# A chunked delta-rule recurrence: the pair's inverse multiplied into B and into the readout's scores once, two product bursts per step

## The chip, the cores and the metric

The kernel runs on one core of one Trainium2 chip. TensorE (PE) multiplies, VectorE (DVE), ScalarE (ACT) and GpSimd (POOL) do the rest, SyncE (SP) issues most transfers. The metric is device time in microseconds (us) of one execution; what counts is the median of several runs.

## The reference

One layer of a hybrid backbone over 256 latent and 256 context tokens, model width 2048, float32. A modulated RMSNorm is followed by one input projection (2048 to 16512 columns); its parts feed a neighbourhood attention, a multi-scale pooling and a bidirectional RWKV-7 mixer, each times a SiLU gate, then through a branch projection, a sigmoid merge gate, one output projection, a gated residual and a last RMSNorm. The change is in the third mixer:

```python
def step(S, inp):                       # 16 heads of 64 x 64, two directions
    rt, vt, wt, kt, at, bt = inp
    sa = jnp.einsum('bhij,bhj->bhi', S, at)
    S = S * wt[:, :, None, :] + sa[..., None] * bt[:, :, None, :] + vt[..., None] * kt[:, :, None, :]
    return S, jnp.einsum('bhij,bhj->bhi', S, rt)
...
y_c, s_ctx_end = wkv_scan(r_c, v_c, *dirs_c[d], s0, reverse=(d == 1))
y_l, _ = wkv_scan(r_l, v_l, *dirs_l[d], s_ctx_end, reverse=(d == 1))
```

The state runs over the 256 context tokens and then over the 256 latent ones; only the latent outputs are used.

## The kernel before, in words

**The dense work.** Weights come as tiles of 512 KB (`raw`, three buffers). ACT rounds half a tile to `whi` (line 576), DVE takes the rest `wlo` (line 577; five buffers of each), and PE multiplies three times for float32 accuracy: columns of the input projection into `d` (line 871; 256 columns wide for latent tokens alone, 512 for both), merge gates and branch projections into `dg` (lines 582 to 584), the output projection into `o`.

**The recurrence** takes two heads at a time, a *pair*, eight pairs in all. Tokens go in chunks of 64: four of the context (q = 0) and four of the latents (q = 1), both directions `d` at once, the two heads as `par`. For each pair `features` makes decays, keys and rates; its scan writes the tile `up` (lines 140, 142), ACT makes exponentials `E` (lines 151 to 154) and `G` (lines 158, 159) of it. `scores` makes the products of the chunks, `inverse` inverts the diagonal blocks of 32 on DVE through a DRAM round trip, and `merge` joins two blocks of 32 to the inverse of 64, `AT` (products `mp`, lines 339 and 347). `chain` then makes eight steps of three bursts of products: `px` (line 374), copied to `xs`; `pu` = inverse times `xs` (line 388), copied to `SV`; and `pS`, the next state (line 398), which DVE multiplies by the decay `G`, with the old state times the decay (`sg`, on POOL). In the four latent steps `py` sums the output from `SV` and state (lines 382, 411). `readout` normalises.

**The order of the work.** PE's order is written out. `Order` runs generators ("streams": one pair's recurrence, attention, pooling, gates); each yields the PE time of what it has just issued and how long its results take, in us, or the name of an event to wait for. Between the bursts of the streams that are ready, `Order.run` puts dense products, at least 0.6 us of them at a time. The next pair's stream is added when this pair's merge has been issued; its second half of features waits for this pair's chain. The other engines' orders follow from the scheduler's priorities. The gate for the residual (`mg`, `pg`, line 1115) is loaded and multiplied near the end; the third branch's projection needs the last pair's output, which goes through DRAM (`bs`, read back as `bh` and `bl`).

**Memory.** PSUM has tags `f` (features, scores; two banks), `m` (merge, `py`, readout; one bank), `c` (chain; one bank), `d` (dense; two) and `s`, `o` (attention). In SBUF the tags `up` and `E` have one buffer each, shared by features, inverse and merge.

Of the kernel before, what the change touches and what calls it, by code (L numbers as in the profile page):

```python
# [9 lines left out]
F32 = mybir.dt.float32  # L10
F32R = mybir.dt.float32r
AF = mybir.ActivationFunctionType
ALU = mybir.AluOpType
# [6 lines left out]
class Rwkv:  # L20
# [90 lines left out]
    def features(s, p, q, zk, zv, T, psp, ptag, gates):  # L111


        nc, fp = s.nc, s.fp
# [11 lines left out]
        k = s.mix(zk, 0, p, "k" + nm)  # L126
# [7 lines left out]
        for d in range(2):  # L134
            nc.scalar.activation(ta[:, d], psa[:, d], AF.Tanh, bias=s.dcol(64 + 8 * d, p), scale=0.5)
        yield 1.0, 2.2

        up = fp.tile([128, 8, 65], F32, tag="up", name=f"up{nm}")
# [9 lines left out]
        h = 0.5 * C  # L148
# [175 lines left out]

    def merge(s, p, psp, ptag):

        nc = s.nc
        at = [s.AT[p, q][:, 0:4].rearrange("p c d t -> p (c d) t") for q in range(2)]
        DN = s.fp.tile([128, 16, 32], F32, tag="up", name=f"DN{p}")
        P = s.fp.tile([128, 16, 32], F32, tag="E", name=f"mP{p}")  # L330
        ps1 = psp.tile([128, 16, 32], F32, tag=ptag, name=f"mp1{p}")
        rr = [(slice(64 * h, 64 * h + 32), slice(64 * h + 32, 64 * h + 64)) for h in range(2)]
        for q in range(2):
            for r1, r2 in rr:
                nc.vector.transpose(DN[r1, 8 * q:8 * q + 8], at[q][r1, :, 0:32])
        yield 0.0, 4.4
        for i in range(16):
            for h, (r1, r2) in enumerate(rr):
                nc.tensor.matmul(ps1[r2, i], at[i // 8][r1, i % 8, 32:64], DN[r1, i], start=True, stop=True,
                                 tile_position=(64 * h, 64 * h + 32))  # L340
        for h, (r1, r2) in enumerate(rr):
            (nc.scalar.copy if h else nc.vector.tensor_copy)(P[r2], ps1[r2])
        yield 0.9, 2.4
        ps2 = psp.tile([128, 16, 32], F32, tag=ptag, name=f"mp2{p}")
        for i in range(16):
            for h, (r1, r2) in enumerate(rr):
                nc.tensor.matmul(ps2[r1, i], P[r2, i], at[i // 8][r2, i % 8, 32:64], start=True, stop=True,
                                 tile_position=(64 * h + 32, 64 * h))
        for q in range(2):
            for h, (r1, r2) in enumerate(rr):  # L350
                (nc.scalar.copy if h else nc.vector.tensor_copy)(at[q][r1, :, 32:64], ps2[r1, 8 * q:8 * q + 8])
        yield 0.9, 2.2

    def chain(s, p, psp, ptag, psy, ytag, y, mark):
        nc = s.nc
        G = s.G[p]
# [4 lines left out]
        for i in range(8):  # L361
            q, w = i // 4, i % 4
            EO, AT, BKT, SV = s.EO[p, q], s.AT[p, q], s.BKT[p, q], s.SV[p, q]
            cs = (w, 3 - w)
            gs = ((i, 0), (i + 1, 1))
            if 0 < i < 7:
                sg = s.fp.tile([128, 2, 64], F32, tag="sg", bufs=2, name=f"sg{p}_{i}")
                for par in range(2):
                    for d in range(2):
                        nc.gpsimd.tensor_scalar(sg[hv[par], d], SV[hv[par], par, w, d], G[hv[par], gs[d][0], d:d + 1], None, ALU.mult)  # L370
            px = psp.tile([128, 2, 64], F32, tag=ptag, name=f"px{p}_{i}")
            for d in range(2):
                for par in range(2):
                    nc.tensor.matmul(px[hv[par], d], EO[:, par, d, cs[d], :], SV[:, par, w, d], start=True, stop=True,  # L374
                                     tile_position=(0, 64 * par))
            xs = s.fp.tile([128, 2, 64], F32, tag="xs", bufs=2, name=f"xs{p}_{i}")
            nc.vector.tensor_copy(xs, px)
            if q:
                py = psy.tile([128, 2, 64], F32, tag=ytag, name=f"py{p}_{i}")
                for d in range(2):  # L380
                    for par in range(2):
                        nc.tensor.matmul(py[hv[par], d], SV[:, par, w, d], EO[:, par, d, 4 + cs[d], :], start=(d == 0), stop=False,
                                         tile_position=(0, 64 * par), skip_group_check=True)
            yield (0.9 if q else 0.45), (1.0 if q else 1.6)
            pu = psp.tile([128, 2, 64], F32, tag=ptag, name=f"pu{p}_{i}")
            for d in range(2):
                for par in range(2):
                    nc.tensor.matmul(pu[hv[par], d], AT[hv[par], cs[d], d, :], xs[hv[par], d], start=True, stop=True)  # L388
            for par in range(2):
                (nc.scalar.copy if par else nc.vector.tensor_copy)(SV[hv[par], par, w], pu[hv[par]])  # L390
            yield 0.4, 2.0
            if i < 7:
# [7 lines left out]
                for par in range(2):  # L400
                    for d in range(2):
                        g = G[hv[par], gs[d][0], d:d + 1]
                        o = SV2[hv[par], par, j % 4, d]
                        if i:
                            nc.vector.scalar_tensor_tensor(o, pS[hv[par], d], g, sg[hv[par], d], ALU.mult, ALU.add)
                        else:
                            nc.vector.tensor_scalar(o, pS[hv[par], d], g, None, ALU.mult)  # L407
# [122 lines left out]
def hybrid_block(ctx, tc, x, cx, w_ms, w_st, w_in, w_mg, w_br, w_out, pool_w, icnt, wa, bias, rows, params, out, dbg=None):  # L530
    nc = tc.nc
# [349 lines left out]
    with ExitStack() as mx:  # L881
# [120 lines left out]
        def rwkv(p):  # L1002
# [20 lines left out]
            yield from R.inverse(p)  # L1023
            yield from R.merge(p, psm, "m")
            if p < 7:
                O.add(rwkv(p + 1), 2 + p + 1)
            if p:
                yield f"rw{p - 1}"
# [83 lines left out]
        def gate_out(cc, gs):  # L1112
            yield 0.0, 4.0
            pg = psn.tile([P, 512], F32, tag="o", name=f"pg{cc}")
# [239 lines left out]
```

## Time and profile before

| | |
|---|---|
| median of 3 runs | 1567.87 us (1566.26 to 1570.13) |
| profiled execution | 1565.28 us, its span 1563.6 us |
| PE busy | 1510.7 us, 97% of the span |
| DVE, ACT, POOL busy | 72%, 51%, 16% |
| granted PE clock | 0.991 of full speed on average |
| HBM traffic | 183 GB/s over the span |

How to read it: a group of instructions stands with its line, its engine, its output and inputs, their shapes, the count, then busy time, mean ns of one, and the idle time before it with what ended it. A float32 product stands as two records in the trace, so four products of a burst read x8. The timeline gives start and duration in us. PE's products are pipelined, so what a product costs is read from one start to the next, not from its duration.

### The profile page before, as it was taken

The numbers are of one execution on the slowest core, as the hardware profiler recorded it, in microseconds if no ns is written. First come the engines' busy times: TensorE is split into PE (matmuls) and PEld (weight loads), VectorE is DVE, ScalarE is ACT, GpSimd is POOL, SyncE is SP. The second block draws the span as 40 slices with busy tenths as digits, with TensorE's granted clock in tenths as the row PEclk, the third lists the DMA queues.
The fourth block names the chain that finished last, engine by engine and source line by source line (L and its number), as shares of the span: only waits on it lengthen the run. The fifth ranks groups of instructions, "written<-read, shape, count | busy, mean of one in ns | idle before, by whom it ended". The sixth has DMA issues, their size and how long they took to land.

```text
span 1563.6 us, 32275 instructions
## 1 busy us (share of the span) xinstructions
PE 1510.7 (97%) x12256; PEld 1199.3 (77%) x12256; DVE 1133.1 (72%) x2602; ACT 798.5 (51%) x1599; POOL 248.5 (16%) x438
## 2 busy tenths in 40 slices
PE   7999999999999999999999999999999999998998
PEld 5667878798877897788789877877896665667787
DVE  5345788788887877886887768778777775566664
ACT  4224663575465546544664556356646633334453
POOL 2332010150022022201230230023023200210000
PEclk9999999999999999999999999999999999999999
DMA  9996445545532464243355524523566698878863
GB/s 391 348 330 223 144 143 169 163 152 179 173 126 91 137 180 147 95 132 122 100 175 159 179 77 132 175 104 118 167 198 211 202 299 274 268 242 262 267 207 111
DMA packets 217811, 288.21 MB, mean 184 GB/s; under 512 B 62516, under 2 KB 176308, under 8 KB 213048
## 3 DMA queue, kind: packets, MB, share of 16 engines
q1 hardware_dynamic: 210160, 275.66, 54.3%
q10 hardware_dynamic: 7496, 10.50, 1.9%
q8 instruction: 96, 1.57, 0.4%
q14 instruction: 59, 0.48, 0.1%
HBM read 264.34 MB, written 21.50 MB: 183 GB/s over the span
## 4 chain that ended last, share of the span: by engine, by line
PE 86%; DVE 5%; DMA 4%; ACT 2%; issue 2%; SPq 0%; ACTq 0%; POOL 0%; DVEq 0%; POOLq 0%
PE d L871 36%; PE dg L582 9%; PE dg L583 7%; PE dg L584 7%; PE acc L793 2%; PE o L582 2%; DMA raw<-in_w_br 2%; PE o L584 2%; PE o L583 2%; PE px L374 2%; PE acc L799 1%; PE acc L796 1%; PE pu L388 1%; PE pS L398 1%; PE psm L693 1%
## 5 line engine op out<-in xcount | busy, mean ns | idle before, releaser
L576 ACT CAST whi<-raw 128x512 fp32r<-128x512 f32 x584 | 354.0, 619 | 388.7 <-PE d L871 169.5
L577 DVE TENSOR_TENSOR wlo<-raw,whi 128x512 fp32r<-128x512 f32 x584 | 400.4, 698 | 131.3 <-ACT whi L576 100.0
L871 PE MATMUL d<-hh,whi 128*128 128x256 f32 (+1 forms) x1184 | 367.5, 330 | 1.1 <-ACT mth L967 1.1
L871 PE MATMUL d<-hl,whi 128*128 128x256 f32 (+1 forms) x1184 | 359.3, 323 | 0.0
L871 PEld LDWEIGHTS d<-hh,whi 128*128 128x128 f32 x1184 | 225.4, 190 | 24.3 <-issue 2.9
L871 PE MATMUL d<-hh,wlo 128*128 128x256 f32 (+1 forms) x1184 | 241.4, 323 | 0.0
L871 PEld LDWEIGHTS d<-hl,whi 128*128 128x128 f32 x1184 | 225.9, 191 | 16.2 <-issue 0.2
L871 PEld LDWEIGHTS d<-hh,wlo 128*128 128x128 f32 x1184 | 183.0, 191 | 16.9 <-issue 0.7
L370 POOL TENSOR_SCALAR sg<-SV,G 64x64 f32<-64x64 f32 x192 | 111.4, 586 | 355.7 <-DVE SV L407 194.1
L582 PE MATMUL dg<-whi,hh 128*128 128x512 f32 x384 | 164.0, 427 | 0.4 <-DVE gnag L911 0.3
L584 PE MATMUL dg<-wlo,hh 128*128 128x512 f32 x384 | 150.7, 392 | 0.8 <-DVE wlo L577 0.6
L583 PE MATMUL dg<-whi,hl 128*128 128x512 f32 x384 | 150.6, 392 | 0.0
L582 PE MATMUL dg<-whi,bh 128*128 128x512 f32 x192 | 83.3, 434 | 10.4 <-ACT whi L576 3.0
L582 PEld LDWEIGHTS dg<-whi,hh 128*128 128x128 f32 x384 | 72.0, 187 | 23.6 <-issue 5.9
L584 PEld LDWEIGHTS dg<-wlo,hh 128*128 128x128 f32 x384 | 72.1, 188 | 17.9 <-DVE wlo L577 1.6
L583 PEld LDWEIGHTS dg<-whi,hl 128*128 128x128 f32 x384 | 72.4, 188 | 10.0 <-issue 0.2
L584 PE MATMUL dg<-wlo,bh 128*128 128x512 f32 x192 | 77.5, 404 | 0.5 <-DVE wlo L577 0.5
L583 PE MATMUL dg<-whi,bl 128*128 128x512 f32 x192 | 77.3, 403 | 0.5 <-DMA bl<-bs 0.5
L309 DVE TENSOR_TENSOR iM<-iA,iT 128x126 f32<-128x126 f32 (+22 forms) x248 | 63.6, 257 | 17.3 <-DMA iA<-dA 10.7
L311 DVE TENSOR_TENSOR iT<-iT,iM 128x126 f32<-128x126 f32 (+22 forms) x248 | 62.8, 253 | 6.6
L806 ACT ACTIVATE hh<-xT,md 128x256 fp32r<-128x256 f32 x32 | 17.5, 593 | 90.5 <-DVE md L717 90.5
L1283 DVE TENSOR_TENSOR wl<-raw,wh 128x512 fp32r<-128x512 f32 x64 | 41.3, 686 | 25.2 <-ACT wh L1282 25.0
(329 smaller groups left out, 2488.6 us busy)
## 6 DMA issues: line engine op xcount, KB each, us to landing
raw<-in_w_in SPq DMA_DIRECT2D x244, 512.0 KB, 3.6
wm<-in_w_ms SPq DMA_DIRECT2D x32, 1024.0 KB, 7.0
raw<-in_w_br SPq DMA_DIRECT2D x48, 512.0 KB, 5.5
wg<-in_w_mg SPq DMA_DIRECT2D x64, 256.0 KB, 4.2
raw<-in_w_out SPq DMA_DIRECT2D x32, 512.0 KB, 4.5
wst<-in_w_st SPq DMA_DIRECT2D x16, 448.0 KB, 7.9
sl<-in_bias SPq DMA_DIRECT2D x32, 128.0 KB, 3.0
iA<-dA SPq DMA_DIRECT2D x16, 256.0 KB, 5.4
```

Source lines behind the costliest of these rows:

```text
L309: nc.vector.tensor_tensor(m, A[:, st:st + 1, st + 1:32].to_broadcast([128, ni, nt]), T[:, 0:ni, st:st + 1].to_broadcast([128, ni, nt]), AL ...
L311: nc.vector.tensor_tensor(T[:, 0:ni, st + 1:32], T[:, 0:ni, st + 1:32], m, ALU.add)
L370: nc.gpsimd.tensor_scalar(sg[hv[par], d], SV[hv[par], par, w, d], G[hv[par], gs[d][0], d:d + 1], None, ALU.mult)
L374: nc.tensor.matmul(px[hv[par], d], EO[:, par, d, cs[d], :], SV[:, par, w, d], start=True, stop=True, tile_position=(0, 64 * par))
L576: nc.scalar.copy(hi, src)
L577: nc.vector.tensor_tensor(lo, src, hi.bitcast(F32), ALU.subtract)
L582: nc.tensor.matmul(acc, a[0], b[0], start=start, stop=False)
L583: nc.tensor.matmul(acc, a[1], b[0], start=False, stop=False)
L584: nc.tensor.matmul(acc, a[0], b[1], start=False, stop=stop)
L793: mm = nc.tensor.matmul(acc[i], shi[:, c], hh[j], start=(j == 0), stop=False)
L871: nc.tensor.matmul(box[0], w[m >= 8][:, 128 * i:128 * i + 128], x, start=(v == 0 and m == 0), stop=(v == 3 and m == 11))
L1283: nc.vector.tensor_tensor(l, r, h.bitcast(F32), ALU.subtract)
```

## The change

`merge` now makes, beside the inverse, the same inverse transposed, as full tiles of 64 x 64 (`An`, 16 a pair): two transposes of 128 partitions on DVE in place of four of 32, two memsets on POOL, and added products (`d2`, `P`) beside the old ones, which one DVE and one ACT copy of 32 x 512 bring to `An`. Then 32 products `pw` a pair multiply `An` into `BKT`, through PSUM tags `m` and `c`, and four copies write `BKT` back. In `chain` the burst `pu` and the copy `xs` are gone: `px` is copied to `SV` directly, and the next state uses the multiplied `BKT`. In the first step 16 products `pz` multiply `An` into the readout's scores `AT[:, 4:8]`, which ACT copies back. `sg` is one product for both directions. The next pair's stream is added before the merge; its features stop after their first part until the merge is issued (`merge{p}`). `gate_out` yields 6.5 us for 4.0. What the yields declare of PE time changes with it.

```diff
+        if q == 0 and p:
+            yield f"merge{p - 1}"
...
-    def merge(s, p, psp, ptag):
+    def merge(s, p, psp, ptag, psc, ctag):
...
-        DN = s.fp.tile([128, 16, 32], F32, tag="up", name=f"DN{p}")
-        P = s.fp.tile([128, 16, 32], F32, tag="E", name=f"mP{p}")
+        An = s.fp.tile([128, 16, 64], F32, tag="E", name=f"An{p}")
+        P = s.fp.tile([128, 16, 32], F32, tag="up", name=f"mP{p}")
...
-                nc.tensor.matmul(ps2[r1, i], P[r2, i], at[i // 8][r2, i % 8, 32:64], start=True, stop=True,
-                                 tile_position=(64 * h + 32, 64 * h))
+                d2 = at[i // 8][r2, i % 8, 32:64]
+                nc.tensor.matmul(ps2[r2, i], d2, P[r2, i], start=True, stop=True, tile_position=(64 * h + 32, 64 * h + 32))
+                nc.tensor.matmul(ps2[r1, i], P[r2, i], d2, start=True, stop=True, tile_position=(64 * h + 32, 64 * h))
+        for h, (r1, r2) in enumerate(rr):
+            (nc.scalar.copy if h else nc.vector.tensor_copy)(An[r2, :, 0:32], ps2[r2])
...
-        yield 0.9, 2.2
+        yield 1.4, 2.4
+        for q in range(2):
+            pw = (psp, psc)[q].tile([128, 2, 4, 64], F32, tag=(ptag, ctag)[q], name=f"pw{p}_{q}")
+            for d in range(2):
+                for c in range(4):
+                    for par in range(2):
+                        nc.tensor.matmul(pw[hv[par], d, c], An[hv[par], 8 * q + 2 * c + d], s.BKT[p, q][hv[par], par, d, c],
+                                         start=True, stop=True)
+            for par in range(2):
+                (nc.scalar.copy if par else nc.vector.tensor_copy)(s.BKT[p, q][hv[par], par], pw[hv[par]])
+        s.An = An
+        yield 1.8, 2.4
...
                 sg = s.fp.tile([128, 2, 64], F32, tag="sg", bufs=2, name=f"sg{p}_{i}")
+                g2 = G.rearrange("p a b -> p (a b)")[:, 2 * i:2 * i + 4:3]
                 for par in range(2):
-                    for d in range(2):
-                        nc.gpsimd.tensor_scalar(sg[hv[par], d], SV[hv[par], par, w, d], G[hv[par], gs[d][0], d:d + 1], None, ALU.mult)
+                    nc.gpsimd.tensor_tensor(sg[hv[par]], SV[hv[par], par, w], g2[hv[par]].unsqueeze(2).to_broadcast([64, 2, 64]), ALU.mult)
...
-            xs = s.fp.tile([128, 2, 64], F32, tag="xs", bufs=2, name=f"xs{p}_{i}")
-            nc.vector.tensor_copy(xs, px)
...
-            yield (0.9 if q else 0.45), (1.0 if q else 1.6)
-            pu = psp.tile([128, 2, 64], F32, tag=ptag, name=f"pu{p}_{i}")
-            for d in range(2):
-                for par in range(2):
-                    nc.tensor.matmul(pu[hv[par], d], AT[hv[par], cs[d], d, :], xs[hv[par], d], start=True, stop=True)
             for par in range(2):
-                (nc.scalar.copy if par else nc.vector.tensor_copy)(SV[hv[par], par, w], pu[hv[par]])
-            yield 0.4, 2.0
+                (nc.scalar.copy if par else nc.vector.tensor_copy)(SV[hv[par], par, w], px[hv[par]])
+            if i == 0:
+                pz = psy.tile([128, 8, 64], F32, tag=ytag, name=f"pz{p}")
+                at = s.AT[p, 1][:, 4:8].rearrange("p c d t -> p (c d) t")
+                for k in range(8):
+                    for par in range(2):
+                        nc.tensor.matmul(pz[hv[par], k], s.An[hv[par], 8 + k], at[hv[par], k], start=True, stop=True)
+                nc.scalar.copy(at, pz)
+            yield (0.9 if q or i == 0 else 0.45), (2.0 if q or i == 0 else 2.3)
...
-            yield from R.merge(p, psm, "m")
             if p < 7:
                 O.add(rwkv(p + 1), 2 + p + 1)
+            yield from R.merge(p, psm, "m", psc, "c")
+            O.mark(f"merge{p}")
...
         def gate_out(cc, gs):
-            yield 0.0, 4.0
+            yield 0.0, 6.5
```

PE's queue from the end of pair 5's merge into its first step, before (left out between the bursts are the dense products `d15` of 128 x 512: twelve, nine and six, the last six around eight of the next pair's features):

```order
L347 MATMUL mp25_12728<-AT5_1_11861,mP5_12612 32x32 x16
...
L374 MATMUL px5_0_12784<-SV5_0_11325,EO5_0_11322 64x64 x4
...
L388 MATMUL pu5_0_12816<-xs5_0_12789,AT5_0_11323 64x64 x4
...
L398 MATMUL pS5_0_12857<-SV5_0_11325,BKT5_0_11324 64x64 x4
```

The same place in the changed kernel; the first and the last of the twelve dense products between the merge and `pw` are shown, and lines count 19 or so higher:

```order
L353 MATMUL mp25_12671<-mP5_12538,AT5_1_11690 32x32
L354 MATMUL mp25_12671<-AT5_1_11690,mP5_12538 32x32
L890 MATMUL d14_12586<-hh7_125,whi567_12560 128x512
...
L890 MATMUL d14_12586<-hl10_144,whi569_12582 128x512
L366 MATMUL pw5_0_12760<-BKT5_0_11188,An5_12537 64x64 x16
L366 MATMUL pw5_1_12779<-BKT5_1_11691,An5_12537 64x64 x16
...
L393 MATMUL px5_0_12817<-SV5_0_11189,EO5_0_11186 64x64 x4
L408 MATMUL pz5_12824<-AT5_1_11690,An5_12537 64x64 x16
...
L417 MATMUL pS5_0_12890<-SV5_0_11189,BKT5_0_11188 64x64 x4
```

`pw` stands where the first `px` stood, twelve dense products behind the merge; `px` and `pz` come another twelve behind it, and the third burst of the step is gone.

DVE's queue at that place, from the first copy out of the merge product (`mp25`), before:

```order
L351 COPY AT5_0_11323<-mp25_12728 32x8x32
L577 TENSOR_TENSOR wlo573_12867<-raw571_12804,whi573_12866 128x512
L351 COPY AT5_1_11861<-mp25_12728 32x8x32
L377 COPY xs5_0_12789<-px5_0_12784 128x128
L577 TENSOR_TENSOR wlo575_12915<-raw574_12912,whi575_12914 128x512
L390 COPY SV5_0_11325<-pu5_0_12816 64x128
L140 TENSOR_SCALAR up6_0_12876<-tw6_0_12848 128x8x64
```

and in the changed kernel, from the first instruction that has to wait for the merge product's end (`up6` takes the buffer of `mP5`):

```order
L142 TENSOR_SCALAR up6_0_12842<-tw6_0_12615 128x8x64
L356 COPY An5_12537<-mp25_12671 32x16x32
L144 SCALAR_TENSOR_TENSOR up6_0_12842<-smask_1438,up6_0_12842 128x520
L596 TENSOR_TENSOR wlo575_12883<-raw574_12880,whi575_12882 128x512
L359 COPY AT5_0_11187<-mp25_12671 32x8x32
L359 COPY AT5_1_11690<-mp25_12671 32x8x32
L369 COPY BKT5_0_11188<-pw5_0_12760 64x512
L369 COPY BKT5_1_11691<-pw5_1_12779 64x512
```

The next pair's first part of the scan (`up6`, lines 142 and 144 of the changed kernel) moved from behind the chain's first copies to between the copies out of the merge product.

PE's queue near the end: the last readout sum of pair 7 and the first product of the third branch (its operand is `bh8`), before, with the twelve dense products between them left out:

```order
L109 MATMUL pvv7_17402<-yv7_1_17358,bones_68 128x256
...
L1115 MATMUL pg3_17433<-gs3_17414,selg_167 128x512
L582 MATMUL dg0_17467<-whi830_17449,bh8_17445 128x512
```

and in the changed kernel, with 99 dense products between them left out:

```order
L109 MATMUL pvv7_17270<-yv7_1_17211,bones_68 128x256
...
L603 MATMUL dg1_17464<-wlo828_17502,bh7_16395 128x512
L601 MATMUL dg0_17554<-whi830_17520,bh8_17356 128x512
```

The last pair's output is made some 90 dense products further ahead of its use, and the last gate product (`pg3`) no longer stands just before it.

More of the change, by code (lines that the diff above doesn't have):

```diff
@@ L323, in inverse @@
         yield 0.0, 10.5
-    def merge(s, p, psp, ptag):
+    def merge(s, p, psp, ptag, psc, ctag):
         nc = s.nc
+        hv = (slice(0, 64), slice(64, 128))
         at = [s.AT[p, q][:, 0:4].rearrange("p c d t -> p (c d) t") for q in range(2)]
-        DN = s.fp.tile([128, 16, 32], F32, tag="up", name=f"DN{p}")
-        P = s.fp.tile([128, 16, 32], F32, tag="E", name=f"mP{p}")
+        An = s.fp.tile([128, 16, 64], F32, tag="E", name=f"An{p}")
+        P = s.fp.tile([128, 16, 32], F32, tag="up", name=f"mP{p}")
         ps1 = psp.tile([128, 16, 32], F32, tag=ptag, name=f"mp1{p}")
@@ L333, in merge @@
         for q in range(2):
-            for r1, r2 in rr:
-                nc.vector.transpose(DN[r1, 8 * q:8 * q + 8], at[q][r1, :, 0:32])
+            nc.vector.transpose(An[:, 8 * q:8 * q + 8], at[q])
+        for r1, r2 in rr:
+            nc.gpsimd.memset(An[r1, :, 32:64], 0.0)
         yield 0.0, 4.4
@@ L338, in merge @@
             for h, (r1, r2) in enumerate(rr):
-                nc.tensor.matmul(ps1[r2, i], at[i // 8][r1, i % 8, 32:64], DN[r1, i], start=True, stop=True,
+                nc.tensor.matmul(ps1[r2, i], at[i // 8][r1, i % 8, 32:64], An[r1, i, 0:32], start=True, stop=True,
                                  tile_position=(64 * h, 64 * h + 32))
@@ L364, in chain @@
             cs = (w, 3 - w)
-            gs = ((i, 0), (i + 1, 1))
             if 0 < i < 7:
                 sg = s.fp.tile([128, 2, 64], F32, tag="sg", bufs=2, name=f"sg{p}_{i}")
+                g2 = G.rearrange("p a b -> p (a b)")[:, 2 * i:2 * i + 4:3]
                 for par in range(2):
-                    for d in range(2):
-                        nc.gpsimd.tensor_scalar(sg[hv[par], d], SV[hv[par], par, w, d], G[hv[par], gs[d][0], d:d + 1], None, ALU.mult)
+                    nc.gpsimd.tensor_tensor(sg[hv[par]], SV[hv[par], par, w], g2[hv[par]].unsqueeze(2).to_broadcast([64, 2, 64]), ALU.mult)
             px = psp.tile([128, 2, 64], F32, tag=ptag, name=f"px{p}_{i}")
@@ L401, in chain @@
                     for d in range(2):
-                        g = G[hv[par], gs[d][0], d:d + 1]
+                        g = G[hv[par], i + d, d:d + 1]
                         o = SV2[hv[par], par, j % 4, d]
```

## The prediction

> **What bounds the kernel now.** I read the page first, then busy time by stages, then the chain of waits in order of time, then PE's own waits and its timeline around single bursts.
>
> ```profile
> span 1563.6 us, 32275 instructions
> PE 1510.7 (97%) x12256; PEld 1199.3 (77%) x12256; DVE 1133.1 (72%) x2602; ACT 798.5 (51%) x1599; POOL 248.5 (16%) x438
> ...
> PE 86%; DVE 5%; DMA 4%; ACT 2%; issue 2%; SPq 0%; ACTq 0%; POOL 0%; DVEq 0%; POOLq 0%
> ```
>
> By stages (us, then PE, PEld, DVE, ACT, POOL busy, then clock, DMA share, GB/s):
>
> ```profile
> 200.00:1200.00 1000.00, 986.65 (x8675) 814.74 (x8674) 795.54 (x1878) 552.78 (x1133) 174.30 (x332) 1.00 0.46 145
> 1200.00:1480.00 280.00, 264.01 (x1852) 188.30 (x1851) 184.90 (x398) 125.57 (x242) 24.59 (x44) 0.98 0.82 259
> ```
>
> From 200 to 1200 us PE lacks 13 of 1000 us: the order in which PE gets its work is written out, and dense products of the weight tiles fill every gap of the recurrence. So a shorter recurrence is worth nothing there by itself; only PE time that disappears, or a new wait, counts. From 1200 on it is different: PE lacks 16 of 280 us, the DMA share is 0.82, and the chain of waits (start, us, what) leaves PE for transfers:
>
> ```profile
> 1116.90 43.85 PE d L871 x312
> ...
> 1354.17 3.81 DMA gs<-in_rows
> ...
> 1414.07 3.46 DMA bs<-kh
> 1418.02 4.88 DMA bl<-bs
> ```
>
> **What PE pays for a product burst.** PE's timeline around one `pu` burst (start, us), one `px` with `py`, and one pair of score tiles:
>
> ```profile
> 604.07 0.39 PE L584 MATMUL dg<-wlo,hh 128*128 128x512 f32 x1
> 604.39 0.45 PE L388 MATMUL pu<-xs,AT 64*64 64x64 f32 x8
> 604.77 0.50 PE L582 MATMUL dg<-whi,hh 128*128 128x512 f32 x1
> 605.11 0.39 PE L583 MATMUL dg<-whi,hl 128*128 128x512 f32 x1
> ...
> 644.77 0.45 PE L374 MATMUL px<-SV,EO 128*64 128x64 f32 x8
> 645.05 0.40 PE L382 MATMUL py<-EO,SV 128*64 128x64 f32 x8
> 645.38 0.96 PE L871 MATMUL d<-hh,wlo 128*128 128x512 f32 x3
> ```
>
> ```profile
> 603.62 0.39 PE L582 MATMUL dg<-whi,hh 128*128 128x512 f32 x1
> 603.84 0.39 PE L583 MATMUL dg<-whi,hl 128*128 128x512 f32 x1
> ```
>
> Dense 512-column products start 0.23 us apart (603.84 to 604.07). From 604.07 to 605.11 two of them should take 0.46; with the burst it is 1.04, so a lone burst of four programmed products (eight records) costs 0.58. Sixteen records last 0.61 from start to the next dense product (644.77 to 645.38), eight last 0.38 (604.39 to 604.77): 0.029 a record, and the other 0.35 is paid for entering and leaving full precision. That 0.35 is what the change saves most often.
>
> **The change, part by part.**
>
> *The `pu` bursts go.* There are 64 (8 pairs, 8 steps). In PE's order 51 stand alone among dense products, 13 beside another full-precision burst. 51 x 0.58 = 29.6; for the 13, which share the switch, between 8 x 0.029 = 0.23 and 0.38, I take 0.30: 3.9. Together -33.5 us. Nothing takes the place of the switches: the other bursts stand as before.
>
> *`pw` is new*: per pair 32 products, 64 records, one burst of its own. They lie as `pu` lies (two positions of the array in turn, 64 columns), so 0.35 + 64 x 0.029 = 2.2 us, 17.7 for eight pairs. The lower bound is a burst that uses four positions:
>
> ```profile
> 622.87 0.27 PE L257 MATMUL pb<-EO,BK 64*64 64x64 f32 x2
> 622.89 0.27 PE L257 MATMUL pk<-EO,BK 64*64 64x64 f32 x2
> ...
> 623.96 0.45 PE L398 MATMUL pS<-SV,BKT 128*64 128x64 f32 x8
> ```
>
> Here 64 records last 1.09 us, 0.017 each, which would make `pw` 0.35 + 1.09 = 1.44, or 11.5 in all. `pw` has only the two positions of `pu`; I take 17.7. *`pz`* stands in the burst of the first `px`: 32 records x 0.029 = 0.93, plus about 0.1 for the changed shape, is 8.2 in all; by 0.017, 4.3.
>
> *The second merge product doubles* (64 to 128 records of 32 columns). The first has
>
> ```profile
> 576.59 1.20 PE L339 MATMUL mp<-DN,AT 32*32 32x32 f32 x64
> 577.72 0.38 PE L871 MATMUL d<-hh,whi 128*128 128x256 f32 x1
> ```
>
> 1.13 us for 64 records at two positions. The added ones have the same rows of the array and other columns, as `pb` and `pk` have: those four run in the time of two. So I take 0 for it; if they take turns, +1.1 a pair, +9 us. The Trainium skill (TensorE: Matmul & The Clock Gate, "Part 3: Packing small matmuls", The mechanism) speaks for the +9: it says a weight load overlaps running products only when it goes to another row group, and the added products share theirs. The `pb` and `pk` rows, which share row groups and start 0.02 us apart, disagree.
>
> PE's own work: -33.5 + 17.7 + 8.2 = **-7.6 us**, with bounds -17.7 (`pw`, `pz` at 0.017) and +1.4 (the merge taking turns).
>
> *A wait before `pw`.* Before, nothing waited soon for the merge's results: `px` came next, in another PSUM tag, and read none of them. Now `pw` reads `An` and its PSUM tile is the bank `m` that the merge product must leave, so it waits for every copy out of it. And because the next pair's features now stand just here, their scan stands between these copies in DVE's queue, and ACT's `G` exponentials, which wait for the scan, stand ahead of ACT's copies. Rows (the tile view gives min/median/max ns, the groups the mean):
>
> ```profile
> L342 DVE COPY mP<-mp 32x512 f32<-32x512 f32 x8 | 5.5, 683 | 7.2 <-PE mp L339 7.1
> L351 DVE COPY AT<-mp 32x256 f32<-32x256 f32 x16 | 6.5, 409 | 4.8 <-PE mp L347 3.4 <-ACT AT L351 1.2
> L140 DVE TENSOR_SCALAR up<-tw x16: 407/427/500, 160.4 to 1218.0; 128x512 f32<-128x512 f32 x16
> L142 DVE TENSOR_TENSOR_SCAN up<-smask,up x16: 1230/1242/1242, 160.9 to 1218.5; 128x520 f32<-128x520 bf16 x16
> L577 DVE TENSOR_TENSOR wlo<-raw,whi 128x512 fp32r<-128x512 f32 x584 | 400.4, 698 | 131.3 <-ACT whi L576 100.0 <-PE d L871 17.6 <-PE dg L583 7.9
> 582.17 0.41 DVE L351 COPY AT<-mp 32x256 f32<-32x256 f32 x1
> ```
>
> In pair 5 DVE's queue after the merge product reads `up` 0.43, `An` 0.68 (priced as the copy of the same shape), scan 1.24, one split 0.70, two `AT` copies 0.82: 3.87, and it starts 0.1 after PE goes on (dense product at 582.05, copy at 582.17). PE has twelve 512-column products to cover it, 12 x 0.23 = 2.76, plus the switches, 3.1. So PE waits 0.9 us. The same count in the other pairs, by the instructions that stand between: 0.4, 1.25, 1.3, 0.9, 2.3, 0.9 and 1.7 for pairs 0 to 6, none in pair 7, which has no next features: **+8.7 us**. It is bounded by 0 (PE arrives later than I count) and about +15 (one more split of 0.70 ahead of each). What is late next is the split of the weights behind these copies; up to five halves are split ahead, so I add nothing.
>
> *Behind such waits the clock may halve.* Stretches around waits of 1.62, 1.36, 2.66 and 2.88 us, the first wait with its row (the clock stands after the busy times):
>
> ```profile
> 1305.79 0.50 PE L582 MATMUL dg<-whi,bh 128*128 128x512 f32 x1 [1.62 <-ACT whi L576]
> ...
> 1306.00:1311.00 5.00, 5.00 (x15) 3.67 (x15) 2.66 (x6) 0.26 (x1) 0.00 (x0) 0.66 0.70 161
> 1316.00:1321.00 5.00, 3.85 (x79) 2.32 (x79) 1.98 (x3) 2.28 (x4) 0.00 (x0) 1.00 1.06 342
> 1357.00:1362.00 5.00, 3.88 (x18) 1.98 (x21) 1.29 (x3) 0.59 (x1) 0.00 (x0) 0.66 0.72 252
> 1422.00:1427.00 5.00, 4.47 (x12) 3.35 (x13) 1.38 (x2) 0.62 (x1) 0.00 (x0) 0.66 0.82 277
> ```
>
> At 0.66 over 5 us, 1.7 us are lost each time. The 1.36 us wait cost none, the other three did. Of my seven, one or two are long enough: **+2**. By the skill's rule (same page, "Part 1: The HAM clock gate") a window of about 3.4 us must be idle first; a wait of 1.62 did it here, so the row decides.
>
> *The end.* The gate product waits for its rows' transfer, and the third branch for the last pair's output:
>
> ```profile
> 1358.12 2.05 PE L1115 MATMUL pg<-gs,selg 128*128 128x512 f32 x2 [2.66 <-DMA gs<-in_rows]
> ...
> 1421.93 0.47 PE L582 MATMUL dg<-whi,bh 128*128 128x512 f32 x1 [2.88 <-DMA bh<-bs]
> 1422.93 0.80 PE L583 MATMUL dg<-whi,bl 128*128 128x512 f32 x1 [0.53 <-DMA bl<-bs]
> ```
>
> With 6.5 for 4.0 the gate product stands 18 to 26 rows behind its sums, not 13 to 16. Between the last readout sum and the third branch's first product PE had 12 dense products, 2.8 us; now it has about 100, some 23 us, for the recurrence ends earlier in PE's order. Both waits should go: 2.66 + 2.88 + 0.53 = 6.1, and the halved clock behind them up to 3.4. Against that, the gate weights (16.8 MB) are asked for later and over a shorter stretch, beside branch weights, at 259 GB/s already. I count **-8** with bounds -9.5 and +5 (the two waits stay and PE lacks a third more of its 16 us).
>
> *Edits that I cost at nothing.* Two groups on DVE and POOL:
>
> ```profile
> L377 DVE COPY xs<-px 128x128 f32<-128x128 f32 x64 | 18.5, 288 | 18.4 <-PE px L374 17.5
> L370 POOL TENSOR_SCALAR sg<-SV,G 64x64 f32<-64x64 f32 x192 | 111.4, 586 | 355.7 <-DVE SV L407 194.1 <-DVE SV L405 152.3
> ```
>
> The `xs` copies leave DVE, 18.5 us, and the copies of `An` and `pw` bring 24 x 0.68 = 16 us there, and with `pz` at most 32 x 0.68 = 22 us to ACT; both engines have idle time under PE (72% and 51% busy). The copy of `px` now overwrites the `SV` that `sg` reads, one burst earlier than before; `sg` took 4 x 0.59 = 2.3 us and is now two instructions, done about when `px` ends; if they were as slow as the four, the copies and with them `pS` would be late by some tenths of a us in 48 steps, up to +10, which I leave to the upper end. `An` keeps the `E` tag until `pz`, so the next pair's four `E` exponentials follow `pz` on ACT; the halves split ahead (2.8 us of PE work each in a wide tile) cover them.
>
> **The sum**: -7.6 + 8.7 + 2 - 8 = -4.9 us, from the profiled execution's 1565.28 us (its span is 1563.6), which is 2.6 under the median of the runs, 1567.87. So **1563 us** against that median. No change cannot be told from 0.3%, 4.7 us, which is where my sum lies.
>
> **The rivals.**
>
> 1. *The waits before `pw` do not come* (chance 0.22): the dense products arrive late enough or DVE has run ahead. For it: PE waited for the first merge copy only 0.4 us in the whole run. Against it: in those places no scan stood in DVE's queue. Then -7.6 - 8 = -16: 1552.
>
> 2. *Slower by the halved clock* (0.17): each of the seven waits before `pw` drops the clock as the waits of 1.6 us and more did. 7 x 1.7 = 12 in place of 2: +5, 1573. It decides once most of them pass about 1.6 us; by my count two do, so one more split ahead of the copies is enough.
>
> 3. *The added merge products take turns* (0.18): the skill's rule above would hold for 32-column products, though not for `pb`. +9 on the sum: +4, 1572; without the waits 1561.
>
> 4. *The change does not shorten the end* (0.13): weight transfers fill the time that the two waits leave. Then -7.6 + 8.7 + 2 = +3: 1571.
>
> **How the numbers follow.** My own case has 0.30, at 1563, with its own range 1558 to 1568; half of it is past 0.3%. Faster: 0.15 + 0.22 + 0.07 (rival 3 without the waits, and rival 1 mixing with 4) = 0.44. Slower: rival 2 0.13, and from 3 and 4 0.09: 0.22. The same: the rest, 0.34. The range runs from rival 1 with some of the lower bounds of `pw` (1549) to rival 2 with 4 (1576).
>
> **What would show it.** Right, if PE's busy groups have no `pu`, a `pw` burst of 2.2 us, an unchanged 1.1 us for the second merge product, and PE's waits name `pw` with DVE or ACT copies of `An` or `AT` for 6 to 12 us. Wrong, if the second merge product lasts 2.2 us, if `pw` waits under 3 us in all, if more than five new stretches at half clock follow those waits, or if PE's lack after 1200 us is not some 6 us smaller.

## The result, and the profile after

The changed kernel takes **1607.08 us** (median of 4 runs, 1601.95 to 1610.5) against 1567.07 for the kernel before (4 runs): a ratio of 1.0253, 95% interval 1.0217 to 1.0289. It is slower by 40 us. Forecast was 1563, with 1576 at the top of the range: the prediction was wrong in its sign. The profiled execution took 1601.95 us, the fastest of the four; the other three had somewhat more halved clock.

The page of the changed kernel: span, busy time of each engine, and the chain that ended last by engine.

```profile
span 1600.2 us, 33713 instructions
PE 1514.4 (95%) x13024; PEld 1215.1 (76%) x13024; DVE 1141.5 (71%) x2546; ACT 819.8 (51%) x1635; POOL 195.5 (12%) x358
...
PE 75%; DVE 10%; DMA 6%; ACT 4%; issue 4%; SPq 1%; ACTq 0%; POOL 0%; DVEq 0%; POOLq 0%
```

PE is as busy as before (1514.4 against 1510.7 us); it is idle for 86 us in place of 53, and DVE, ACT and transfers have a larger part in the chain. The same two stages as in the prediction:

```profile
200.00:1200.00 1000.00, 955.91 (x9032) 796.34 (x9030) 773.68 (x1778) 552.91 (x1125) 115.10 (x248) 0.99 0.44 137
1200.00:1480.00 280.00, 264.36 (x2087) 196.74 (x2088) 191.83 (x403) 127.89 (x253) 30.66 (x48) 0.98 0.78 247
```

From 200 to 1200 us PE lacks 44 us where it lacked 13. From 1200 to 1480 it lacks 16, as before. PE's waits from 200 to 1200 us (engine, line, who ended it, us in all, times, longest), of the kernel before and then of the changed one:

```profile
PE pS L398 <- ACT SV L390: 3.0, 2, 1.8
PE S L1057 <- DVE gnag L1086: 2.8, 1, 2.8
PE pk L259 <- DVE EO L277: 1.8, 2, 1.4
```

```profile
PE pw L366 <- issue: 14.0, 6, 2.8
PE S L1077 <- DVE gnag L1106: 5.1, 2, 2.7
PE dg L603 <- DVE wlo L596: 3.7, 6, 1.0
```

Two things are to be seen: one large new wait, before `pw`, and many small ones that have nothing to do with the recurrence's new products (`S` is attention, `dg` dense work). Over the whole span the group has

```profile
L366 PE MATMUL pw<-BKT,An 64*64 64x64 f32 x512 | 20.0, 243 | 17.3 <-issue 16.3 <-ACT AT L359 1.0
```

17.3 us before eight bursts ("issue" means that the profile names nobody who ended a wait; who did is read from the timeline below). A balance over the span can be made from the page: idle is the span less PE's busy time; the time lost at half clock is (1 - mean clock) x span, 14 before (0.991) and 21 after (0.987); what is left of busy time is *work*, 1497 and 1494, each uncertain by some 0.8 through the rounding of the clock. So 36.6 us of span = **33 of idle + 7 of halved clock - 3 of work**.

### The profile page after: what moved, and what is told of

Same layout as the page of the kernel before. It is cut to its first block, busy times and chain, and to the rows that moved or that the text cites. A ratio compares the mean times of both kernels' runs of the same rounds, so it can differ in the third digit from the quotient of the medians.

```text
span 1600.2 us, 33713 instructions
## 1 busy us (share of the span) xinstructions
PE 1514.4 (95%) x13024; PEld 1215.1 (76%) x13024; DVE 1141.5 (71%) x2546; ACT 819.8 (51%) x1635; POOL 195.5 (12%) x358
## 4 chain that ended last, share of the span: by engine, by line
PE 75%; DVE 10%; DMA 6%; ACT 4%; issue 4%; SPq 1%; ACTq 0%; POOL 0%; DVEq 0%; POOLq 0%
PE d L890 30%; PE dg L601 7%; PE dg L603 6%; PE dg L602 6%; DVE wlo L596 3%; DMA raw<-in_w_br 2%; PE o L601 2%; PE acc L812 2%; PE o L603 2%; PE o L602 2%; PE acc L818 1%; PE acc L815 1%; PE px L393 1%; PE pw L366 1%; PE pS L417 1%
## 5 line engine op out<-in xcount | busy, mean ns | idle before, releaser
L389 POOL TENSOR_TENSOR sg<-SV,G 64x128 f32<-64x128 f32 x96 | 51.2, 533 | 192.1 <-DVE SV L424 148.2
```

The lines of the kernel that those rows point to most:

```text
L389: nc.gpsimd.tensor_tensor(sg[hv[par]], SV[hv[par], par, w], g2[hv[par]].unsqueeze(2).to_broadcast([64, 2, 64]), ALU.mult)
```

## The experiments

All ratios are against the kernel before, run beside each. Idle and work are those of the profiled execution, worked out as above.

| kernel | median us | ratio [95%] | idle | work |
|---|---|---|---|---|
| before | 1567.07 | 1 | 53 | 1497 |
| changed kernel | 1607.08 | 1.0253 [1.0217, 1.0289] | 86 | 1494 |
| no dead copies | 1586.15 | 1.0118 [1.0081, 1.0155] | 73 | 1495 |
| longer cover before `pw` | 1583.48 | 1.0107 [1.0078, 1.0136] | 68 | 1490 |
| merge in two banks | 1589.9 | 1.0143 [1.0122, 1.0164] | 77 | 1492 |
| later stream | 1601.61 | 1.0228 [1.0170, 1.0285] | 86 | 1485 |
| before + earlier stream | 1584.42 | 1.0115 [1.0086, 1.0144] | 69 | 1503 |
| no dead copies, later stream | 1591.02 | 1.0145 [1.0112, 1.0177] | 79 | 1488 |
| before, features 2.6 for 2.2 | 1583.81 | 1.0103 [1.0073, 1.0134] | 66 | 1499 |
| before, `pu` 2.3 for 2.0 | 1585.42 | 1.0106 [1.0077, 1.0134] | 69 | 1501 |
| before, inverse 10.9 for 10.5 | 1568.78 | 1.0006 [0.9988, 1.0023] | 54 | 1497 |
| before, gate 6.5 for 4.0 | 1564.67 | 0.9991 [0.9970, 1.0012] | 51 | 1498 |
| no dead copies + cover 4.0 | 1574.07 | 1.0037 [1.0019, 1.0055] | 63 | 1490 |
| the same, cover 3.4 | 1575.59 | 1.0041 [1.0025, 1.0058] | 59 | 1489 |
| cover 4.0, first merge product 3.2 | 1572.52 | 1.0029 [1.0017, 1.0042] | 59 | 1491 |
| the same, gate 4.0 again | 1575.43 | 1.0045 [1.0027, 1.0062] | 61 | 1491 |
| no dead copies, both merge products in two banks | 1564.93 | 0.9978 [0.9957, 0.9998] | 58 | 1492 |
| the same, step's latency 2.3 | 1567.11 | 0.9977 [0.9957, 0.9998] | 61 | 1493 |

### The wait before `pw`

The prediction had priced DVE's queue. The timeline of DVE and ACT in pair 3 of the changed kernel, between the second merge product and `pw` (start, us):

```profile
729.75 0.68 DVE L356 COPY An<-mp 32x512 f32<-32x512 f32 x1
...
730.46 1.39 DVE L144 TENSOR_TENSOR_SCAN up<-smask,up 128x520 f32<-128x520 bf16 x1
...
730.52 0.58 ACT L356 COPY An<-mp 32x512 f32<-32x512 f32 x1 [2.69 <-DVE An L356]
...
731.88 0.41 DVE L359 COPY AT<-mp 32x256 f32<-32x256 f32 x1
731.89 0.21 ACT L160 ACTIVATE G<-up 128x4 f32<-128x4 f32 x1 [0.79 <-DVE up L144]
...
732.10 0.60 ACT L595 CAST whi<-raw 128x512 fp32r<-128x512 f32 x1
732.73 0.36 ACT L359 COPY AT<-mp 32x256 f32<-32x256 f32 x1
732.74 0.69 DVE L596 TENSOR_TENSOR wlo<-raw,whi 128x512 fp32r<-128x512 f32 x1 [0.44 <-ACT whi L595]
733.34 0.41 DVE L359 COPY AT<-mp 32x256 f32<-32x256 f32 x1
733.78 0.36 ACT L359 COPY AT<-mp 32x256 f32<-32x256 f32 x1 [0.69 <-DVE AT L359]
...
734.25 2.08 PE L366 MATMUL pw<-BKT,An 64*64 64x64 f32 x64 [2.06 <-issue]
```

The copies of DVE and ACT do not run beside each other: ACT's `An` waits for DVE's and starts 0.09 after its end, ACT's last `AT` waits 0.69 for DVE's. All six come out of one PSUM bank. So they form one chain over both engines, 0.68 + 0.58 + 2 x (0.41 + 0.36) = 2.8 us without anything between, and whatever stands between them on *either* engine (scan, `G`, cast, split) comes on top: from 729.75 to 734.14. In all eight pairs `pw` starts 0.10 to 0.15 us after ACT's last copy of `AT`. The view of line 359 gives how long one engine sat idle for the other (us, times):

```profile
  DVE AT L359: 6.6, 12
  ACT AT L359: 2.6, 6
```

The copies of `AT` have a second peculiarity: since `pu` is gone, nothing reads what they write (the inverse in the first four chunks of `AT`) any more. They and the products that make them are dead work that the change left in place. **Without them:**

```diff
-                nc.tensor.matmul(ps2[r1, i], P[r2, i], d2, start=True, stop=True, tile_position=(64 * h + 32, 64 * h))
...
-        for q in range(2):
-            for h, (r1, r2) in enumerate(rr):
-                (nc.scalar.copy if h else nc.vector.tensor_copy)(at[q][r1, :, 32:64], ps2[r1, 8 * q:8 * q + 8])
```

> The changed kernel without the four copies a pair of the merge product into the inverse (AT, chunks 0 to 3) and the 32 products that make that half; nothing reads them any more. Two theories of the 40 us. THE COPY CHAIN: DVE and ACT copy out of one PSUM bank in turns (An, An, AT, AT, AT, AT: 0.68 + 0.58 + 2 x (0.41 + 0.36) = 2.8 us, with scan, G and splits between them), and pw waits for the last; without the four AT copies the chain is 1.3 us, so PE's waits before pw fall from 17 us to under 6, and with some of the halved clock behind them the time falls by 12 to 20, to 1587 to 1595. EARLY FEATURES: the time goes to the next pair's features, which now load DVE and ACT beside merge and chain; then pw's waits matter little and the time stays above 1598.

Measured: 1586.15, that is 21 us off, as the chain of copies said. PE's order is otherwise the same in both traces: of its 7232 records that are neither `d` nor `dg` nor the products left out, none stands behind another number of `d` and `dg` products than in the changed kernel. So the 21 us belong to the copies and not to another order. `pw` waits 4.4 us:

```profile
PE pw L362 <- ACT An L355: 2.4, 2, 2.0
PE pw L362 <- issue: 2.0, 1, 2.0
```

**One number of latency**, so that PE has more dense products to do there:

```diff
-        yield 1.4, 2.4
+        yield 1.4, 5.0
```

> The changed kernel with one number changed: the merge yields 5.0 us of latency for 2.4 before pw, so PE gets some 2.6 us more of dense products there. THE COPY CHAIN: the waits before pw (17 us) go, and the halved clock behind them: 1607 - 17 - 4 = 1586 (1582 to 1592). EARLY FEATURES: the splits of the weights are what is late; more dense products there only take the splits that the next burst would have needed, waits move to wlo and whi: 1600 or more.

Measured: 1583.48, again as the chain of copies said, though this number moves three quarters of PE's other records (5812 of 7744) among the dense products as well. `pw` waits 2.9 us, though some wait moved to the splits (10.3 us for `whi`, where 1.9 stood).

**Are the turns at the bank the cause, or what stands in the queues?** The same copies from two banks (`h` is the half that ACT copies):

```diff
-        ps2 = psp.tile([128, 16, 32], F32, tag=ptag, name=f"mp2{p}")
+        ps2 = [(psp, psc)[h].tile([128, 16, 32], F32, tag=(ptag, ctag)[h], name=f"mp2{p}_{h}") for h in range(2)]
```

> The changed kernel with the second merge product in two PSUM banks, the half that DVE copies in one (tag m) and the half that ACT copies in the other (tag c); same products, same copies, same yields. TURNS AT ONE BANK: the copies stop waiting for each other; DVE's three take 1.5 us and ACT's three 1.3 beside them instead of 2.8 in all, so the waits before pw fall from 17 us to about 7 and the time by 10 to 15, to 1592 to 1597. THE QUEUES (scan, exponentials and splits stand between the copies and would stand there still): 3 us at most, 1603 or more.

Measured: 1589.9, 17 us off, somewhat more than expected, and with PE's order unchanged (of 7744 records none moved; DVE's and ACT's orders differ in 47 places each). At the place shown above, DVE and ACT now start together, and the row of `pw`'s waits names DVE:

```profile
730.87 0.68 DVE L356 COPY An<-mp 32x512 f32<-32x512 f32 x1 [0.43 <-PE mp L354]
730.92 0.58 ACT L356 COPY An<-mp 32x512 f32<-32x512 f32 x1 [1.48 <-PE mp L354]
```

```profile
PE pw L366 <- DVE AT L359: 7.4, 6, 1.8
```

From 17.3 to 8.2 (0.8 more stands in a row of its own). In the seven pairs that still wait, `pw` now starts 0.15 us after DVE's last copy, and ACT's last is done 1.8 us or more before. In pair 7, which has no next features and waited 2.3 us before, the wait is gone. So the turns make about half of the wait, and DVE's own queue (its copies, the scan, the splits) the rest, which is the part that the prediction had counted (8.7).

The Trainium skill (PSUM — Partial Sum Buffer, "PSUM bank collisions raise a hardware error") says that two engines may not touch one bank in the same 32 partitions at once, but may in different ones. DVE and ACT copied from different 32 partitions here and waited all the same; so by that page the turns are put there by the program's guard on the whole bank and not by the chip. No run here has both engines reading one bank at once, so this stays the page's word.

### The earlier stream

**The changed kernel with the next pair's stream behind the merge**, as before the change:

```diff
-        if q == 0 and p:
-            yield f"merge{p - 1}"
...
-            if p < 7:
-                O.add(rwkv(p + 1), 2 + p + 1)
             yield from R.merge(p, psm, "m", psc, "c")
-            O.mark(f"merge{p}")
+            if p < 7:
+                O.add(rwkv(p + 1), 2 + p + 1)
```

> The changed kernel, with the next pair's stream added behind the merge as before (no features between the merge's copies); An, pw, pz and the two-burst step stay. THE COPY CHAIN: pair 7 has no next features and its pw waited 2.3 us, so the waits stay at 10 us or more and only the scan and the G exponentials leave them: 1607 - 5 to 8 = 1599 to 1602. EARLY FEATURES: scan, exponentials and BK products go back to where dense work covers them; 20 to 30 us come back: 1577 to 1587.

Measured: 1601.61, a gain of 5 us that its interval does not tell from none, and far from the 1577 to 1587 of the early features. The waits before `pw` do fall, to 7.7 us, below the 10 that the chain of copies had; but the last pair now comes 25 us later (its `pw` at 1376 us, not 1351), and the third branch waits 5.1 us for its output (`bh` from `bs`).

**The kernel before with the earlier stream alone** (the same lines put in, nothing else):

> The kernel before with only the earlier stream: the next pair's stream is added before the merge and its features stop until the merge is issued; no An, pw, pz, three bursts a step, gate yield 4.0. THE COPY CHAIN: nothing waits soon for the merge's copies here, so no change, 1567 within 4 us. EARLY FEATURES: 15 us or more slower, 1582 and above, with new waits on wlo, whi and on the gates' copies.

Measured: 1584.42, 18 us slower than the kernel before beside it, where the chain of copies had no change and the early features 15 us or more. So here the earlier stream costs time, and the trace shows a part of how. `pS`, the state product, waits for ACT's copy of `pu`:

```profile
PE pS L400 <- ACT SV L392: 8.9, 7, 1.8
```

Before, this was 3.0 us in two places (line 398). In all seven places the square root of the next pair's features (line 174) stands just ahead of that copy in ACT's queue, and with it the load of its table. One of them:

```profile
1041.62 1.28 ACT L174 ACT_TABLE_LOAD   x1
1042.92 0.42 ACT L174 ACTIVATE n<-n 128x256 f32<-128x256 f32 x1
1043.36 0.26 ACT L392 COPY SV<-pu 64x128 f32<-64x128 f32 x1
...
1043.67 0.45 PE L400 MATMUL pS<-SV,BKT 128*64 128x64 f32 x8 [1.81 <-ACT SV L392]
```

In the changed kernel `pS` waits 1.7 us in all, and never behind that load: this cost did not pass over to it. **Both parts together** (no dead copies, later stream) are a second test there:

> The changed kernel without the dead AT copies and products, and with the next pair's stream added behind the merge as before. If the two parts add, 1607 - 21 (no dead copies) - 5 (later stream) = 1581; as the later stream already takes some of the waits before pw, 1583 to 1590 is likelier. THE EARLIER STREAM (18 us slower alone on the kernel before) as a cost of its own: 1570 or less.

Measured: 1591.02, no better than with the earlier stream (1586). So with the two-burst step no run shows a cost of the earlier stream. It is not excluded either, since putting the stream back moves three quarters of PE's other records as well (5890 of 7744 with the dead copies, 5378 of 7232 without). The sum of the two gains, 1581, was missed: the two do not add.

### The order itself

With each edit of the streams PE's order is worked out anew: the earlier stream alone moved 3262 of 6976 records of the kernel before. To see what that is worth by itself, the kernel before was changed in **one number each**, without a single instruction more or less: the latency that the first part of the features declares (2.6 for 2.2), that of `pu` (2.3 for 2.0), that of the inverse (10.9 for 10.5), and the gate's (6.5 for 4.0, the piece of the change that was meant for the end).

```diff
-        yield 1.0, 2.2
+        yield 1.0, 2.6
```

> The kernel before with one number changed that adds and removes no instruction: the first part of the features yields 2.6 us of latency for 2.2, so every later burst of the recurrence may stand elsewhere among the dense products. THE TUNED ORDER: 8 to 20 us slower, 1574 to 1586, by scattered waits of PE and perhaps some halved clock. The rival, THAT THE NEW WORK COSTS (An, pw, pz, the earlier features): 1567 within 4.

> The kernel before with another single number changed and no instruction added: the burst pu yields 2.3 us of latency for 2.0. THE TUNED ORDER (the order before is a good draw among many; any shift gives an ordinary one, with 10 to 15 us more of scattered waits): 1575 to 1590. ITS RIVAL, that the first part of the features is a delicate place and the other shift (1584) was special: 1567 within 5.

> The kernel before, a third single number: the inverse yields 10.9 us of latency for 10.5. THE TUNED ORDER: 1573 to 1590. ITS RIVAL: 1567 within 5, since the inverse waits for a round trip through DRAM and 0.4 us there is little.

> The kernel before with the gate's yield 6.5 for 4.0 alone. THE END'S WAITS GO, as the prediction has it: gate-row wait 2.66 and perhaps the halved clock behind it, 1562 to 1565. THE TUNED ORDER: the gate weights come later and something else is short by as much: 1566 to 1575.

Measured: 1583.81, 1585.42, 1568.78 and 1564.67. The first two are what a tuned order would give; the third is not, but it moved far less. Counted in the traces, of PE's 6976 records that are neither `d` nor `dg`, 4796, 4672, 1512 and 16 stand behind another number of those than in the kernel before. The two that moved two thirds cost 16 to 18 us; the two that moved 22% and 0.2% cost nothing that can be measured. The two largest waits behind the start, in the first one, are 6.0 us for `bh` and 5.6 for `whi`. The waits are in all parts of the program: 5.5 of 13 us of its additional idle time lie from 200 to 1200 us, the rest behind. A longer latency also ends the recurrence later (`bh` 6.0, and 7.8 with the change to `pu`, for 2.9), so 3 to 5 of the 16 us follow from that and not from the order; most of the others are waits of 1 to 3 us at places that were covered before. The kernel before stands at a place of its latencies where nearly everything is covered; the two orders that moved most do not. No run shortened a latency.

The gate alone gains nothing that can be measured: the waits for `gs` and `bh` are gone, and PE waits 8.2 us for the splits of the weights (`whi`) instead of 3.0.

### The change without its waits

Three kernels without the dead copies, with latencies fitted by hand to the copies that are left, one number at a time (`yield 0.9, 4.0` before `pw`; 3.4 there; 4.0 and 3.2 behind the first merge product), then the last of them with the gate's yield at 4.0 again:

> The changed kernel without the dead AT copies and products, and with a yield of 0.9 and 4.0 before pw. THE COPY CHAIN alone accounts for some 22 us of the 40: what is left of PE's waits before pw (4.4 us) goes, 1580 to 1583, and no further. THE TUNED ORDER (a new theory for the rest: the latencies that set PE's order were fitted to the order before, so any change that shifts the streams leaves PE short in new, scattered places): the same or worse, 1580 to 1592, with waits in other places than the two parents had.

> The changed kernel without the dead copies and products, yield 0.9 and 3.4 before pw (4.0 gave 1574). THE TUNED ORDER: an ordinary draw of a program with some 8 us less PE work than the kernel before: between 1568 and 1585. THE COPY CHAIN is still short of cover at 3.4: pw waits of 2 to 4 us in all come back, 1578.

> The changed kernel without the dead copies and products, yield 0.9 and 4.0 before pw, and 3.2 for 2.4 after the first merge product, whose copies also take turns (its two long waits were 4.9 us in the last run). THE COPY CHAIN: these waits go with a half-clock stretch, 1574 - 5 to 8 = 1566 to 1569. THE TUNED ORDER: they go, and as much comes elsewhere: 1568 to 1582.

> The last kernel (no dead copies, yields 3.2 and 4.0 in the merge: 1572.5) with the gate's yield at 4.0 again. THE LATER GATE costs something at the end (a wait of 4.0 us for the gate weights with 10 us of halved clock behind it stands there in every kernel with 6.5 and the shorter step): 1562 to 1568. THE DRAW OF THE ORDER: the gate alone moved nothing on the kernel before, so 1570 to 1576.

Measured: 1574.07, better than either theory had, then 1575.59, 1572.52 and 1575.43, all three in the ranges of an ordinary draw of the order. What is left to the kernel before, 5 to 8 us, does not go with any one of them. The wait for the gate weights, with its halved clock, stays whatever the gate's yield is (4.0 us with 6.5, 3.8 with 4.0), so the later gate is not its cause.

**Both merge products in two banks**, without the dead copies, and with the shorter latencies that this allows (2.4 and 3.0):

> The same kernel (gate yield 6.5) with both merge products in two banks and with the yields that the shorter copies need, 2.4 and 3.0 for 3.2 and 4.0. TURNS AT ONE BANK: no wait over 1 us before pw or behind the first merge product in spite of the shorter yields; the time is that of lean_c or less, 1565 to 1573. THE QUEUES: waits of 4 us or more come back, 1576 or more.

Measured: **1564.93, ratio 0.9978 [0.9957, 0.9998]**. Nothing waits before `pw` any more, the mean clock is 0.993, and the first stage is

```profile
200.00:1200.00 1000.00, 978.06 (x8984) 816.95 (x8984) 798.70 (x1828) 564.61 (x1152) 129.67 (x273) 0.99 0.46 142
```

The last pair's last state product stands at 1361 us, 25 earlier than in the kernel before (1386). PE still lacks 22 us in the first stage where the kernel before lacks 13. **One latency more** (2.3 us behind the copies of `px` in the latent steps and the first one):

> The fastest kernel so far (two banks in the merge, no dead copies: 1564.9) with 2.3 for 2.0 us of latency behind the copies of px in the latent steps and the first step, where py and pS waited some 5 us in all. THE COVER: these waits go, 1558 to 1563. THE DRAW OF THE ORDER: an ordinary draw, the same waits elsewhere, 1565 to 1577.

Measured: 1567.11, ratio 0.9977 [0.9957, 0.9998] against a kernel before that took 1570.18 beside it. Its waits lie elsewhere (11.8 us for `whi`, and 2.4 before one `pw`), as the draw of the order said. So the new algebra comes out 0.2% ahead once its waits are away. That is the edge of what was measured, and these two are the fastest of eight kernels without the dead copies; besides, the second bank is no part of the new algebra and was not tried on the kernel before. That the algebra alone gains is therefore not shown.

## Why the prediction was wrong

**What bounds the kernel** was read rightly: dense products fill PE, and a shorter recurrence is worth nothing by itself. The chain's state products of pair 5 take 42 us where they took some 51 (1046 to 1088 in the changed kernel, 1030 to 1081 before), and the time grew.

**PE's own work** (-7.6) was about right. One `pw` burst without a wait, in the kernel without dead copies, beside one `px` with `pz` in the changed kernel:

```profile
730.68 0.39 PE L886 MATMUL d<-hh,wlo 128*128 128x512 f32 x1
731.00 2.08 PE L362 MATMUL pw<-BKT,An 64*64 64x64 f32 x64
733.01 0.50 PE L886 MATMUL d<-hh,whi 128*128 128x512 f32 x1
733.35 0.39 PE L886 MATMUL d<-hl,whi 128*128 128x512 f32 x1
```

```profile
739.21 0.45 PE L393 MATMUL px<-SV,EO 128*64 128x64 f32 x8
739.59 1.15 PE L408 MATMUL pz<-AT,An 64*64 64x64 f32 x32
740.67 0.39 PE L108 MATMUL psn<-sq,bones 128*128 128x256 f32 x1
```

733.35 - 730.68 - 2 x 0.23 = 2.2 us for `pw`, as taken; 740.67 - 739.59 = 1.08 for `pz` (1.03 taken). The doubled merge product was taken at nothing:

```profile
727.96 0.21 PE L353 MATMUL mp<-mP,AT 32*32 32x32 f32 x1
727.96 0.21 PE L354 MATMUL mp<-AT,mP 32*32 32x32 f32 x1
...
729.17 0.50 PE L890 MATMUL d<-hh,whi 128*128 128x512 f32 x1
```

1.21 us for 128 records where 64 took 1.13, so rival 3 (some 1.1 us more a pair) falls. The Trainium skill (TensorE: Matmul & The Clock Gate, "Part 3: Packing small matmuls", The mechanism) says that weight loads overlap running products only when the row group differs; this trace disagrees, for the added products share their row groups and cost 0.08 us. In the table, work is 1497 to 1503 (mean 1499) with the three-burst step and 1485 to 1495 (mean 1491) with the two-burst step: 8 us less. The two profiled executions differ by 3 alone: the kernel before has the lowest value of its kind and the changed one nearly the highest. So the 8 us lean on the means, and on the two bursts priced above. Whether the 0.35 us of a lone burst is the price of full precision, as the prediction has it, or of the small tiles, no run here tells.

**The wait before `pw`** (+8.7, bound +15) was the right place with the wrong size: 17.3. The step that failed is the count "by the instructions that stand between" in *DVE's* queue alone. ACT's copies come in turns with DVE's, and what stands in ACT's queue counts too; pair 7, put at none, waited 2.3. The bound was one more split, on the same wrong chain. Rival 1 (no such waits) falls with it. The runs give 17 to 24 us back when this wait is shortened or covered, its halved clock among them.

**The halved clock** (+2): in the stretches around three of the eight `pw` waits the clock is 0.66 over 5 us, a loss of 1.7 each:

```profile
442.00:447.00 5.00, 3.03 (x71) 2.91 (x72) 2.61 (x6) 1.81 (x6) 0.00 (x0) 1.00 0.01 3
881.00:886.00 5.00, 2.91 (x56) 2.94 (x58) 1.85 (x4) 1.10 (x5) 0.00 (x0) 0.66 0.37 117
1035.00:1040.00 5.00, 4.34 (x68) 4.07 (x69) 1.52 (x3) 0.94 (x2) 0.00 (x0) 0.66 0.01 3
1185.00:1190.00 5.00, 4.70 (x72) 3.87 (x73) 1.58 (x3) 1.36 (x3) 0.00 (x0) 0.66 0.31 98
```

Pair 1 (442 us) waited 2.43 us and kept its clock. The three make 5 us, not the 12 of rival 2, which falls; with the other new waits 7 in all.

**The end** (-8) did not come: PE lacks 16 us from 1200 to 1480 as before. The stretch holds other work in the two kernels; over the same dense products (from the one at 1200 us in the kernel before to the output projection) PE's idle time is 16.0 and 15.6 us. The waits for `bh`, `bl` and `gs` went, as predicted, and others came; the two longest are

```profile
PE mg L1158 <- DMA wg<-in_w_mg: 3.3, 1, 3.3
PE dg L601 <- DVE gnag L930: 2.6, 1, 2.6
```

The step that failed is that a wait which goes leaves nothing in its place. The gate's yield alone shows the same on the kernel before: -0.09%. Rival 4's result (the end is not shortened) came true; that transfers fill the time is not shown by it, since the waits that came name DVE and ACT as often.

**Edits at nothing.** The step of the recurrence gave no trouble: `pS` waits 1.7 us in all for the copies of `px`, where it waited 3.0 for those of `pu`, so the upper bound of 10 for `sg` was not used. "What is late next is the split ... so I add nothing" is the step that hid the rest: from 200 to 1200 us idle time grew by 31, and 15 of these stand before `pw`. The other 16 lie in small waits, which no single edit accounts for. They have nothing to do with the copies: beside the waits before `pw`, PE lacks 29 us in this stage in the changed kernel, 29 without the dead copies and 30 with the merge in two banks, for 13 before. The first two changed numbers in the kernel before, with no work added, make 6 and 11 us of them in the same stage (PE busy 981.13 and 975.85 of 1000 us). The prediction treated the order outside the edited places as fixed; a change of the declared times can move most of it. None of the four rivals had this. It is the missing case, and no row of one profile gave its price, 16 to 18 us where two thirds of the kernel before moved. (The top of the range has a slip of its own: rivals 2 and 4 together come to 1581 by the prediction's terms, not 1576.)

So where did the 40 us go? Term by term, forecast and then what the profiled executions show: PE's work -7.6 and -3; the wait before `pw` +8.7 and +17; halved clock +2 and +7; the end -8 and 0; all else 0 and some +16. The copies between merge and step are the largest part, and shown: with PE's order untouched, the runs give 21 and 17 us back. The scattered waits are the rest. That a new order brings such waits is shown on the kernel before, 16 to 18 us without any new work; that those of the changed kernel come from its order is argued by that likeness and not shown. The later kernels, 33 us back with cover and 42 with both merge products in two banks, have new orders as well, so how much of their gain is cover and how much the draw is not settled.

## What to carry to other kernels

When a new consumer is put right behind a product, price the way out of PSUM as one chain over all engines that copy from that bank, with everything that stands in each of their queues, and ask whether each copy is still read by anyone. Where an order is worked out from declared times, an edit that changes one of them can draw a new order (the single numbers tried here moved from 0.2% to 75% of PE's other records); measure a kernel with one such number nudged before believing that a difference of 1% belongs to the edit, and prefer tests that leave the order as it is. A saving should be judged after the declared times have been fitted again.

## What was not expected of the hardware

Added 32 x 32 products on the same rows of the array and other columns cost next to nothing: 0.08 us for 64 more records. And the halved clock does not follow from the length of a wait alone: 2.43 us before the `pw` of pair 1 left the clock at 1.00, and 2.09 before that of pair 5 were followed by a halved one (rows above, at 442 and 1035 us). What else decides is open.
